# Layer 1 of a hybrid decoder step: transposed queries and keys leave PSUM in one copy

## The chip, the cores and the metric

The kernel runs on one core of a Trainium2 chip. The metric is the device time of one execution in microseconds. Four engines do the work here: TensorE (PE, with its weight loads shown as PEld), VectorE (DVE), ScalarE (ACT) and GpSimd (POOL); the queue of SyncE (SP) issues the DMAs. Matmul results land in PSUM, which ACT and DVE read; everything else lives in SBUF.

## The reference, cut to what matters

Layer 1 is stick-breaking attention with 16 heads of width 64 over 1024 prompt tokens (and 8 samples of 8 tokens, which go another way and matter little here).

```
u = h @ w_in
q = rms_norm(u[..., :SB_W].reshape(bsz, length, SB_HEADS, SB_DH), qn)
k = rms_norm(u[..., SB_W:2 * SB_W].reshape(bsz, length, SB_HEADS, SB_DH), kn)
...
z = jnp.einsum('bqhd,bkhd->bhqk', qi, k).astype(jnp.float32) * (dh ** -0.5) + bias_f
valid = k_pos[None, :] < pi[:, None]
log_1mb = jnp.where(valid, jax.nn.log_sigmoid(-z), 0.0)
rest = lax.cumsum(log_1mb, axis=3, reverse=True)
a = jnp.exp(jnp.where(valid, z + rest, -jnp.inf))
return jnp.einsum('bhqk,bkhd->bqhd', a.astype(v.dtype), v)
...
return (o * jax.nn.silu(g)) @ w_out, k, v
```

Every matmul operand is split into a high part in fp32r and a low part, the rest of it, so that products come out near full fp32 accuracy. Making such parts is what the code of this change does.

## The kernel before

Layer 0 takes the first 535 us, layer 1 the rest. Layer 1 goes over 8 pairs of heads (p = 0 to 7), and in each pair over four blocks of 256 tokens (m = 0 to 3). For each pair and block it does, on different engines at once:

- The projection of two row tiles of 128 tokens to this pair's q, k and v columns (`dense`, line 293, into PSUM tile `acc`), and of the gate columns (`dense_t`, line 315). ACT squares q and k (`sq`, L799) and copies v (L801), DVE sums (`ms`, L802), POOL takes the power -1/2 (`rs`, L804), and DVE scales q and k out of `acc` into SBUF (`qk`, L810), which frees `acc` for the next tile.
- `qk_p`, once per block: PE transposes q and k of both row tiles into a PSUM tile `tr` of 128x512 (L829). Then ten operations read `tr`: ACT makes four pieces of the queries' high part `qh` (L853, four operations on 64 partitions) and two pieces of the keys' high part into `kc` (L854, L855); DVE makes the two pieces of the queries' low part `ql` (L856, L857) and the two low pieces of the keys in `kc` (L858, L859). The function runs 32 times.
- The attention units, two heads by m + 1 key blocks: logits `z` on PE (L881), two sigmoids on ACT (`om` L884, `A` L885), on diagonal units a masking on POOL (L890), the running products by a scan on DVE (`run`, L908) and a product (L913 or L916). Then `A` is transposed by PE into another `tr` tile (L932), copied out as high part by ACT (`aT`, L934) and low part by DVE (L935), and multiplied with v on PE (`o`, L944).
- `gate_b`, once per block: it adds the two halves of `o` (ACT copies one half to `sh`, L954; DVE adds, L955, into `og`) and POOL multiplies with the gate (L956).
- The weights of the next pair: DMA into a ring of three raw tiles `wr`, high part on ACT or DVE (L219, L221), low part on POOL (L222). This falls into block 3 of a pair.

Each of the PSUM tiles `acc`, `tr`, `z` and `o` has two buffers. The order of the matmuls on PE is written by hand, by the times given to a timeline; the order on ACT, DVE, POOL and SP is made by a scheduler from the dependencies. Each engine runs its own queue strictly in order, so an instruction that waits holds all behind it.

Of the kernel before, what the change touches and what calls it, by code (L numbers as in the profile page):

```python
# [9 lines left out]
F32 = mybir.dt.float32  # L10
# [3 lines left out]
AF = mybir.ActivationFunctionType  # L14
# [62 lines left out]
def tile_hybrid_decoder(ctx, tc, x_prompt, x_sample, state_gla, cache_k, cache_v, page_table,  # L77
# [3 lines left out]
    nc = tc.nc  # L81
# [46 lines left out]
    def sb(pool, name, shape, dtype=F32, bufs=2, tag=None):  # L128
        return pools[pool].tile(shape, dtype, name=name, tag=tag or name, bufs=bufs)
# [532 lines left out]
    for h in range(GH):  # L662
# [3 lines left out]
        for c, (c_0, n) in enumerate(CH):  # L666
            st = {}
            G.append(st)
            if h == 0:
                a, b = QK0[c]  # L670
                la = LA0[c]
            else:
                a, b = i, i + 1
# [5 lines left out]
            for j, (key, out) in enumerate((("q", q_out), ("k", k_out))):  # L679
                lo, hi = a + (b - a) * 0.5 * j, a + (b - a) * 0.5 * (j + 1)  # L680
                dense_t(lo, hi, c_0, n, wqk,
                        lambda w, k, j=j: (w[k // 2], slice((k % 2) * 256 + j * 128, (k % 2) * 256 + j * 128 + 128)),
# [84 lines left out]
    K1 = {}  # L767
# [59 lines left out]
    def turn_qk(st, n, tr, slots):  # L827
        for j, x in enumerate(slots):
            nc.tensor.transpose(tr[:, x, :n], st["qk"][:n, 2 * j:2 * j + 2].rearrange("p a d -> p (a d)"), ident[:n, :n])  # L829
# [7 lines left out]
    def qk_p(sts, pair):  # L837

        tr = psum.tile([128, 4, 128], F32, name="tr")
        for x, st in enumerate(sts):
            turn_qk(st, 128, tr, (x, 2 + x))
        tr = tr.rearrange("p a s -> p (a s)")
        qp, kp, g = tr[:, :256], tr[:, 256:], K1["gains"]
        qh, kc = sb("at2", "qh", [128, 2, 256], F32R, NQ), sb("at2", "kc", [128, 2, 256], F32R, NKV)
        ql = K1["ql"][K1["turn"] % NQ]
        K1["turn"] += 1
        pair["q"].append((qh, ql))
        pair["k"].append(kc)  # L850
        up, dn = slice(0, 64), slice(64, 128)
        for dst, j, src in ((up, 0, up), (dn, 1, dn), (dn, 0, up), (up, 1, dn)):
            nc.scalar.activation(qh[dst, j], qp[src], AF.Copy, scale=g[src])  # L853
        nc.scalar.activation(kc[up, 0], kp[up], AF.Copy)  # L854
        nc.scalar.activation(kc[dn, 1], kp[dn], AF.Copy)  # L855
        nc.vector.scalar_tensor_tensor(ql[up, 0], qp[up], g[up], qh[up, 0], op0=OP.mult, op1=OP.subtract)  # L856
        nc.vector.scalar_tensor_tensor(ql[dn, 1], qp[dn], g[dn], qh[dn, 1], op0=OP.mult, op1=OP.subtract)  # L857
        nc.vector.tensor_sub(kc[dn, 0], kp[up], kc[up, 0])  # L858
        nc.vector.tensor_sub(kc[up, 1], kp[dn], kc[dn, 1])  # L859
# [87 lines left out]

    def gate_b(q, pair, p, m):
        po = q["po"]
        sh, og = sb("at2", "sh", [128, 256], F32, 1), sb("at2", "og", [128, 256], F32, 2)  # L950
        q["og"] = og
        for j in range(2):
            main, other = slice(64 * j, 64 * j + 64), slice(64 - 64 * j, 128 - 64 * j)
            nc.scalar.activation(sh[main], po[other, j], AF.Copy)  # L954
            nc.vector.tensor_add(og[main], po[main, j], sh[main])  # L955
        nc.gpsimd.tensor_mul(og, og, pair["g"][m])  # L956

    def tps(m):
# [30 lines left out]
    for p in range(PAIRS):  # L989
# [4 lines left out]
        def columns(t, i, span):  # L994
            st = {}
            dense(i, t, w, st, span, 384)
            e = i + span
            at(e + 0.02, qk_sums, st, p, t)
            at(e + C_SC, qk_scale, st, p, t)
            sts.append(st)  # L1000
            if t < NP:
                at(max(e + C_SC, open2), v_parts, st, t, pair)
            if t == NP:
                at(e + C_TS, qk_s, st, p)
            elif t % 2 == 1:
                at(max(e + C_T, open2 + 0.01 * t), qk_p, sts[t - 1:], pair)
            at(max(e + C_T, open2) + 0.2, kv_store, st, p, t)
            return e
# [8 lines left out]
        for m in range(NP // 2):  # L1017
            i = columns(2 * m, i, 0.75)
            i = columns(2 * m + 1, i, 0.75)
            ready = max(i + UNIT0, open2 + 0.5)  # L1020
            if m < NP // 2 - 1:
                i = gates(m, i, 0.5)
            else:
                i = gates(m, i, 0.625)
                i = columns(NP, i, 0.5)
            q = {}
            units = [(j, c) for j in range(2) for c in range(m, -1, -1)]
            for x, (j, c) in enumerate(units):
                u = {}
                z0 = max(free, ready)  # L1030
                free = z0 + PACE
                at(z0, logits, u, pair, p, m, c, j)
                at(z0 + L_STICK, stick, u, pair, m, c, j)
                at(z0 + L_TURN, turn, u, m, c)
                at(z0 + L_AV, weigh, u, q, pair, c, j, x == 0, x == len(units) - 1)
            at(z0 + L_AV + 0.05, gate_b, q, pair, p, m)
            at(z0 + L_AV + 0.35, store_b, q, p, m)
            if p == PAIRS - 1:
                st = {}
                for g in range(4):  # L1040
                    n = 2 if g < 3 else 1
                    at(i + 0.1 + 0.05 * g, load_h, st, m, g, n)
                    at(i + 0.6 + 0.05 * g, take_h, st, m, g, n)
# [203 lines left out]
```

## Time and profile before

| what | value |
|---|---|
| runs before, median (range), n = 3 | 1372.65 us (1367.76 to 1372.9) |
| the profiled execution, its own time | 1375.27 us |
| its span in the profile | 1373.6 us |
| busy, PE / PEld | 1282.8 us (93%) / 1140.3 us (83%) |
| busy, DVE / ACT / POOL | 1012.5 us (74%) / 709.7 us (52%) / 587.0 us (43%) |
| DMA | 115.82 MB, mean 84 GB/s |

The busy shares are means over the whole run. PE is the busiest engine in every stage; what a change in layer 1 is worth is read from what PE waits for there, and from what the other engines wait for just before.

### The profile page before, as it was taken

The numbers are of one execution on the slowest core, as the hardware profiler recorded it, in microseconds if no ns is written. First come the engines' busy times: TensorE is split into PE (matmuls) and PEld (weight loads), VectorE is DVE, ScalarE is ACT, GpSimd is POOL, SyncE is SP. The second block draws the span as 40 slices with busy tenths as digits, with TensorE's granted clock in tenths as the row PEclk, the third lists the DMA queues.
The fourth block names the chain that finished last, engine by engine and source line by source line (L and its number), as shares of the span: only waits on it lengthen the run. The fifth ranks groups of instructions, "written<-read, shape, count | busy, mean of one in ns | idle before, by whom it ended". The sixth has DMA issues, their size and how long they took to land.

```text
span 1373.6 us, 23656 instructions
## 1 busy us (share of the span) xinstructions
PE 1282.8 (93%) x8025; PEld 1140.3 (83%) x8025; DVE 1012.5 (74%) x2047; ACT 709.7 (52%) x1640; POOL 587.0 (43%) x1101
## 2 busy tenths in 40 slices
PE   6999999999999998989989899898998989989998
PEld 5788888888878788989889898898998988877666
DVE  7858759668564457788888988789788898986443
ACT  6446245352441134566756667566666667763221
POOL 6223223223231216465655846557466574543000
PEclk9999999999999999999999999999999999999999
DMA  6311402304246423020110201102012022134762
GB/s 195 92 32 43 137 20 68 108 32 133 91 129 213 145 101 104 18 81 18 58 42 22 79 17 55 47 24 80 16 41 63 23 89 68 32 121 155 249 245 88
DMA packets 118459, 115.82 MB, mean 84 GB/s; under 512 B 11003, under 2 KB 97923, under 8 KB 118339
## 3 DMA queue, kind: packets, MB, share of 16 engines
q1 hardware_dynamic: 118338, 114.31, 27.2%
q8 instruction: 64, 1.05, 0.3%
q14 instruction: 57, 0.46, 0.1%
HBM read 83.61 MB, written 30.67 MB: 83 GB/s over the span
## 4 chain that ended last, share of the span: by engine, by line
PE 55%; DVE 18%; POOL 9%; ACT 7%; issue 7%; DMA 3%; SPq 1%; POOLq 0%; ACTq 0%; DVEq 0%
PE acc L293 31%; PE acc L315 7%; DVE run L908 4%; PE z L881 3%; PE tr L932 3%; PE o L944 2%; POOL wlo L222 2%; POOL rs L804 2%; ACT qh L853 2%; DVE whi L221 2%; PE o L544 1%; DVE aT L935 1%; DVE wr L217 1%; POOL v L819 1%; PE o L1154 1%
## 5 line engine op out<-in xcount | busy, mean ns | idle before, releaser
L293 PE MATMUL acc<-whi,h 128*128 128x512 f32 (+1 forms) x1728 | 538.7, 374 | 10.1 <-DVE qk L810 7.9
L293 PEld LDWEIGHTS acc<-whi,h 128*128 128x128 f32 x1728 | 313.5, 189 | 41.1 <-ACT sh L954 4.2
L293 PE MATMUL acc<-wlo,h 128*128 128x512 f32 (+1 forms) x864 | 322.5, 373 | 3.9 <-DVE wlo L222 2.5
L315 PE MATMUL acc<-h,whi 128*128 128x256 f32 (+5 forms) x832 | 193.5, 318 | 10.3 <-DVE g L512 5.1
L222 POOL TENSOR_TENSOR wlo<-wr,whi 128x512 fp32r<-128x512 f32 x98 | 139.1, 1422 | 123.5 <-DVE whi L221 93.2
L293 PEld LDWEIGHTS acc<-wlo,h 128*128 128x128 f32 x864 | 162.8, 188 | 22.7 <-DVE wlo L222 3.2
L908 DVE TENSOR_TENSOR_SCAN run<-om,run 128x256 f32<-128x256 f32 x192 | 146.7, 802 | 11.0 <-ACT om L884 10.5
L315 PEld LDWEIGHTS acc<-h,whi 128*128 128x128 f32 (+2 forms) x832 | 141.3, 189 | 15.1 <-DVE g L512 6.0
L934 ACT ACTIVATE aT<-tr 128x512 fp32r<-128x512 f32 (+1 forms) x160 | 88.9, 556 | 103.9 <-PE tr L932 90.2
L884 ACT ACTIVATE om<-z,bias 128x512 f32<-128x512 f32 (+1 forms) x160 | 103.3, 646 | 52.6 <-PE z L881 43.1
L932 PE MATMUL tr<-ident,A 128*128 128x128 f32 x576 | 91.5, 277 | 39.3 <-POOL v L819 18.3
L315 PE MATMUL acc<-h,wlo 128*128 128x256 f32 (+2 forms) x392 | 123.8, 316 | 0.5 <-POOL wlo L222 0.5
L293 PE MATMUL acc<-w,h 128*128 128x384 f32 (+1 forms) x480 | 122.6, 365 | 0.7 <-DVE qk L810 0.7
L932 PEld LDWEIGHTS tr<-ident,A 128*128 128x128 f32 x576 | 69.5, 142 | 55.1 <-POOL run L903 19.4
L935 DVE TENSOR_TENSOR aT<-tr,aT 128x512 fp32r<-128x512 f32 (+1 forms) x160 | 100.8, 630 | 9.1 <-ACT aT L934 6.8
L944 PE MATMUL o<-aT,v 128*128 128x256 f32 x640 | 105.0, 286 | 0.0
L885 ACT ACTIVATE A<-z,bias 128x512 f32<-128x512 f32 (+1 forms) x160 | 102.4, 640 | 0.0
L944 PEld LDWEIGHTS o<-aT,v 128*128 128x128 f32 x640 | 97.2, 194 | 1.8 <-DVE aT L935 1.1
L908 DVE TENSOR_TENSOR_SCAN run<-om 128x128 f32<-128x128 f32 (+1 forms) x128 | 85.0, 695 | 13.6 <-POOL om L890 13.6
L881 PE MATMUL z<-kc,qh 128*128 128x256 f32 x320 | 86.1, 290 | 7.3 <-DVE kc L858 7.3
L804 POOL TENSOR_TENSOR rs<-ms,half_exp 128x4 f32<-128x4 f32 (+1 forms) x72 | 83.9, 1166 | 20.3 <-DVE ms L802 18.8
L293 PEld LDWEIGHTS acc<-w,h 128*128 128x128 f32 x480 | 82.2, 189 | 7.2 <-issue 2.5
(274 smaller groups left out, 2531.7 us busy)
## 6 DMA issues: line engine op xcount, KB each, us to landing
wr<-in_w_in_b_dram SPq DMA_DIRECT2D x64, 256.0 KB, 3.0
wr<-in_w_in_a_dram SPq DMA_DIRECT2D x32, 256.0 KB, 3.2
kp<-in_cache_k_dram SPq DMA_DIRECT2D x16, 512.0 KB, 5.0
vp<-in_cache_v_dram SPq DMA_DIRECT2D x16, 512.0 KB, 4.5
o_d<-og SPq DMA_DIRECT2D x60, 128.0 KB, 1.8
x<-in_x_prompt_dram SPq DMA_DIRECT2D x8, 512.0 KB, 4.8
wr<-in_w_in_a_dram SPq DMA_DIRECT2D x32, 128.0 KB, 3.7
n<-in_state_gla_dram SPq DMA_DIRECT2D x8, 512.0 KB, 3.9
```

Source lines behind the costliest of these rows:

```text
L222: engine.tensor_sub(e.lo[:, :m], raw[:, :m], e.hi[:, :m])
L293: nc.tensor.matmul(st["ps"][:x.shape[1], :n], x, (w[k].hi if part == 0 else w[k].lo)[:, :n], start=first, stop=last)
L315: nc.tensor.matmul(st[key][:x.shape[1], :n], x, y, start=first, stop=last)
L804: nc.gpsimd.tensor_tensor(st["rs"][:n], ms[:n], half_exp[:n], op=OP.pow)
L881: nc.tensor.matmul(out, lhs, rhs, start=x == 0, stop=x == len(mm) - 1)
L884: nc.scalar.activation(u["om"][:, v0:], z[:, v0:], AF.Sigmoid, scale=-1.0, bias=K1["bias"][:, 1, hd:hd + 1])
L885: nc.scalar.activation(u["A"][:, v0:], z[:, v0:], AF.Sigmoid, bias=K1["bias"][:, 0, hd:hd + 1])
L908: nc.vector.tensor_tensor_scan(run[:, a, n - 1::-1], rev, rev, init, op0=OP.mult, op1=OP.bypass)
L932: nc.tensor.transpose(tr[:, x], u["A"][:, col:col + 128], ident)
L934: nc.scalar.activation(hi[:, v0:], tr[:, v0:], AF.Copy)
L935: nc.vector.tensor_sub(lo[:, v0:], tr[:, v0:], hi[:, v0:])
L944: nc.tensor.matmul(q["po"][:, j], vs, part[:, x * 256:(x + 1) * 256], start=first and n == 0, stop=last and n == 3)
```

## The change

`qk_p` copies the whole `tr` tile once to an SBUF tile `both` on ACT, and the ten operations read `both`. To make room in SBUF, `gate_b` loses its tile `sh`: ACT copies the half of `o` straight into `og`, and DVE adds in place.

```diff
@@ qk_p
         for x, st in enumerate(sts):
             turn_qk(st, 128, tr, (x, 2 + x))
-        tr = tr.rearrange("p a s -> p (a s)")
-        qp, kp, g = tr[:, :256], tr[:, 256:], K1["gains"]
+        both = sb("at2", "both", [128, 512], F32, 1)
+        nc.scalar.activation(both, tr.rearrange("p a s -> p (a s)"), AF.Copy)
+        qp, kp, g = both[:, :256], both[:, 256:], K1["gains"]
@@ gate_b
-        sh, og = sb("at2", "sh", [128, 256], F32, 1), sb("at2", "og", [128, 256], F32, 2)
+        og = sb("at2", "og", [128, 256], F32, 2)
         q["og"] = og
         for j in range(2):
             main, other = slice(64 * j, 64 * j + 64), slice(64 - 64 * j, 128 - 64 * j)
-            nc.scalar.activation(sh[main], po[other, j], AF.Copy)
-            nc.vector.tensor_add(og[main], po[main, j], sh[main])
+            nc.scalar.activation(og[main], po[other, j], AF.Copy)
+            nc.vector.tensor_add(og[main], po[main, j], og[main])
```

Lines behind the diff's first place are one higher in the changed kernel (L856 becomes L857, L932 becomes L933, and so on). The order of PE's 6801 instructions does not change.

On ACT, in the third block of a pair, the queue reads as follows before the change; what stands in brackets are the engines whose semaphores an instruction waits for.

```order
L885 ACTIVATE A<-z,bias 128x512
L853 ACTIVATE qh<-tr,gains 64x256 [waits PE_49]
L853 ACTIVATE qh<-tr,gains 64x256 x3
L854 ACTIVATE kc<-tr 64x256
L855 ACTIVATE kc<-tr 64x256
L934 ACTIVATE aT_7570<-tr 128x384 [waits PE_49,Activation_49,Pool_49]
```

And with the change:

```order
L886 ACTIVATE A<-z,bias 128x512
L845 ACTIVATE both<-tr 128x512 [waits PE_49]
L854 ACTIVATE qh<-both,gains 64x256 [waits Activation_49]
L854 ACTIVATE qh<-both,gains 64x256 x3
L855 ACTIVATE kc<-both 64x256
L856 ACTIVATE kc<-both 64x256
L935 ACTIVATE aT_7579<-tr 128x384 [waits PE_49,Pool_49]
```

One instruction is added ahead of the six, and the first of the six waits for it.

On DVE, at the same place, the first `ql` waits for ACT and the other three behind it for nothing further before the change:

```order
L916 TENSOR_TENSOR A<-A,run 128x512 [waits DVE_49,Activation_49,Pool_49]
L856 SCALAR_TENSOR_TENSOR ql_5786<-tr,gains,qh 64x256 [waits PE_49,Activation_49]
L857 SCALAR_TENSOR_TENSOR ql_5786<-tr,gains,qh 64x256
L858 TENSOR_TENSOR kc<-tr,kc 64x256
L859 TENSOR_TENSOR kc<-tr,kc 64x256
L935 TENSOR_TENSOR aT_7571<-tr,aT_7570 128x384 [waits Activation_49]
```

With the change each of the four has a wait of its own:

```order
L917 TENSOR_TENSOR A<-A,run 128x512 [waits DVE_49,Activation_49,Pool_49]
L857 SCALAR_TENSOR_TENSOR ql_5786<-both,gains,qh 64x256 [waits Activation_49]
L858 SCALAR_TENSOR_TENSOR ql_5786<-both,gains,qh 64x256 [waits Activation_49]
L859 TENSOR_TENSOR kc<-both,kc 64x256 [waits Activation_49]
L860 TENSOR_TENSOR kc<-both,kc 64x256 [waits Activation_49]
L936 TENSOR_TENSOR aT_7580<-tr,aT_7579 128x384 [waits Activation_49]
```

On PE, in the last block of a pair, the second transpose of an `A` behind a `qk_p` (the one that gets its buffer of `tr` back) reads so before:

```order
L932 MATMUL tr<-ident,A 128x128 [waits DVE_49,PE_49,Pool_49]
L932 MATMUL tr<-ident,A 128x128 x2
```

And with the change:

```order
L933 MATMUL tr<-ident,A 128x128 [waits DVE_49,Activation_49,Pool_49]
L933 MATMUL tr<-ident,A 128x128 x2
```

It now waits for ACT as well; DVE and POOL stay, since `A` comes from there.

## Rows read from the trace of the kernel before

**Rows 1.** Who waited for whom, PE, 535 to 1260 us: total, times, longest.

```profile
PE tr L932 <- POOL v L819: 18.3, 6, 3.1
PE tr L932 <- DVE kc L859: 11.9, 8, 1.8
PE acc L293 <- DVE qk L810: 8.6, 10, 1.7
PE z L881 <- DVE kc L858: 7.3, 10, 1.4
PE tr L932 <- ACT sq L799: 4.5, 7, 0.9
```

**Rows 2.** Who waited for whom, DVE, the same stretch.

```profile
DVE ql L856 <- ACT kc L855: 45.8, 24, 4.7
```

**Rows 3.** Timeline, block 0 of pair 3: start, us, instruction, [idle before it].

```profile
793.29 1.92 ACT L853 ACTIVATE qh<-tr,gains 64x256 fp32r<-64x256 f32 x4 [1.32 <-PE tr L829]
...
795.61 0.38 ACT L855 ACTIVATE kc<-tr 64x256 fp32r<-64x256 f32 x1
...
796.01 0.60 ACT L934 ACTIVATE aT<-tr 128x512 fp32r<-128x512 f32 x1
796.02 0.48 DVE L856 SCALAR_TENSOR_TENSOR ql<-tr,gains,qh 64x256 fp32r<-64x256 f32 x1 [2.38 <-ACT kc L855]
...
797.45 0.43 DVE L859 TENSOR_TENSOR kc<-tr,kc 64x256 fp32r<-64x256 f32 x1
...
797.90 0.69 DVE L935 TENSOR_TENSOR aT<-tr,aT 128x512 fp32r<-128x512 f32 x1
798.02 0.63 PE L932 MATMUL tr<-ident,A 128*128 128x128 f32 x4 [0.58 <-ACT sq L799]
```

**Rows 4.** Timeline, block 2 of the same pair.

```profile
833.89 0.38 ACT L854 ACTIVATE kc<-tr 64x256 fp32r<-64x256 f32 x1
...
835.71 0.42 DVE L858 TENSOR_TENSOR kc<-tr,kc 64x256 fp32r<-64x256 f32 x1
...
836.27 0.36 PE L881 MATMUL z<-kc,qh 128*128 128x256 f32 x1 [0.56 <-DVE kc L858]
```

**Rows 5.** Timeline, block 3 of the same pair.

```profile
854.13 1.32 POOL L222 TENSOR_TENSOR wlo<-wr,whi 128x512 fp32r<-128x512 f32 x1
854.24 0.47 DVE L856 SCALAR_TENSOR_TENSOR ql<-tr,gains,qh 64x256 fp32r<-64x256 f32 x1
...
855.66 0.42 DVE L859 TENSOR_TENSOR kc<-tr,kc 64x256 fp32r<-64x256 f32 x1
...
856.23 0.52 PE L932 MATMUL tr<-ident,A 128*128 128x128 f32 x3 [1.46 <-DVE kc L859]
...
856.77 1.30 POOL L222 TENSOR_TENSOR wlo<-wr,whi 128x512 fp32r<-128x512 f32 x1 [1.17 <-ACT whi L219]
...
857.18 2.07 DVE L908 TENSOR_TENSOR_SCAN run<-om,run 128x256 f32<-128x256 f32 x2
```

**Rows 6.** Timeline at the end of the same block 3.

```profile
871.02 0.87 PE L932 MATMUL tr<-ident,A 128*128 128x128 f32 x3 [3.06 <-POOL v L819]
```

**Rows 7.** Instructions of ACT by shape: busy us, mean ns, idle before.

```profile
L1110 ACT ACTIVATE KT<-tr 128x512 f32<-128x512 f32 x16 | 9.6, 598 | 31.3 <-PE tr L1107 31.2
...
L965 ACT ACTIVATE h<-og 128x256 fp32r<-128x256 f32 x4 | 1.7, 418 | 1.5 <-POOL og L956 1.5
```

**Rows 8.** Busy us from 815.30 to 825.50, by engine: PE, PEld, DVE, ACT, POOL.

```profile
815.30:825.50 10.20, 10.11 (x74) 9.79 (x74) 9.96 (x23) 6.70 (x16) 6.99 (x18) 1.00 0.10 31
```

**Rows 9.** Line 810, all: ns min/median/max, first and last start.

```profile
L810 DVE TENSOR_TENSOR qk<-acc,rs x64: 393/425/426, 527.6 to 1195.9; 128x256 f32<-128x256 f32 x64
...
L810 DVE TENSOR_TENSOR qk<-xr,rs x8: 406/1172/1178, 600.8 to 1215.2; 64x256 f32<-64x256 f32 x8
```

**Rows 10.** The page's group of full scans on DVE (busy us, mean ns).

```profile
L908 DVE TENSOR_TENSOR_SCAN run<-om,run 128x256 f32<-128x256 f32 x192 | 146.7, 802 | 11.0 <-ACT om L884 10.5
```

**Rows 11.** Who waited for whom, PE, 1255 us to the end.

```profile
PE tr L1107 <- DMA kp<-in_cache_k_dram: 3.8, 4, 1.8
```

## The prediction

> **What bounds the kernel now.** I read the busy shares first. PE is the busiest engine over the run (93%), so the matmuls alone would take most of the time, and the change leaves their number and order as they are. What it can move is the time in which PE waits, in layer 1 alone. So the second view is who waited for whom, on PE, over layer 1 [rows 1]. Its five largest lines add up to 50.6 us in some 725, and two of them name the low key pieces of `qk_p` outright: 11.9 us in which a transpose waits for L859, and 7.3 us in which logits wait for L858. A third, 4.5 us in seven waits, names ACT's `sq`, and here the reader should look closer. In the timeline of that place [rows 3] PE starts the transposes at 798.02. They need a free `tr`, and the last reader of the buffer that comes round is L859, which ends at 797.88, 0.14 us before. In blocks 2 and 3, where the view names L858 and L859, PE starts 0.14 and 0.15 us behind them [rows 4, 5]. `sq` has nothing to do with `tr`; it only ended a moment later. So all three lines, 23.7 us, hang on `qk_p`.
>
> The third view is DVE's own waits. Its largest by far is the first `ql`, 45.8 us in 24 waits, for ACT's last key piece [rows 2]. That is odd, since `ql` needs only the first piece of `qh`. In block 0 the six ACT pieces run from 793.29 to 795.99, and `ql` starts 0.03 us behind the last of them, after 2.38 us of idling [rows 3]. DVE does not read `tr` while ACT does. [...] So the ten readers of `tr` are one chain of some 4.6 us (793.29 to 797.88), and the buffer is taken throughout.
>
> **The change, part by part.**
>
> The copy. It has the shape of L1110, a 128x512 fp32 copy out of PSUM: 0.60 us [rows 7]. The six pieces behind it then read SBUF. The nearest row is L965, 128x256 from SBUF, 0.418 us [rows 7], against 0.38 for a key piece [rows 3]. That is up to 0.04 us more for each, 0 to 0.24 us for six; I take 0.15, and 0.03 for the first one's wait for the copy, as `ql` shows it for another engine. ACT's key pieces, and everything behind them on ACT, come 0.8 us later (bounds 0.6 and 0.9). For ACT that is 32 x 0.8 = 26 us more work at a busy share of 52%.
>
> `tr` is free 0.60 us after the transposes instead of 4.6. The seven waits of block 0 go: PE comes to them at 798.02 - 0.58 = 797.44, and the buffer is free at 793.9. Gain 4.5 us.
>
> The logits of block 2. Each DVE piece now waits for its own ACT piece alone, as the order shows. The first ACT key piece ends at 834.27 [rows 4]; 0.8 later is 835.07, the DVE piece starts 0.03 behind it and ends at 835.52, against 836.13 now: 0.61 us earlier, enough for the wait of 0.56. Of the ten waits I take seven as of this size, 3.9 us, and let the three that share the other 3.4 us gain no more than 0.61 each. Gain 5.7 us.
>
> DVE behind the pieces, in blocks 0 and 1. Its next instruction (L935) needs ACT's `aT`, which ends 0.8 us later, at 797.41, and the last DVE piece, which ends at 795.99 + 0.8 + 0.03 + 0.43 = 797.25. So it starts at 797.44 and not at 797.90, 0.46 us earlier. In block 1 DVE then has no rest for ten microseconds (9.96 of 10.20 us busy [rows 8]), up to the sums that lead to `qk`, for which PE waits 8.6 us in ten waits [rows 1]. I take 0.4 us for eight of them, 3.2 us; bounds 0 and 4.6.
>
> The last block is different. There DVE does not wait for ACT: it comes to `ql` late, at 854.24, without idling, while POOL works on weights [rows 5]. The wait of 1.46 us goes from the transposes, but DVE is what is late, and PE then waits for its next products, and again 3.06 us at the block's end [rows 6]. I count none of the 11.9 us; the upper bound is half of it, 6 us.
>
> And there is a cost. The four DVE pieces so far have one input in PSUM, and ran at 0.42 to 0.49 us beside POOL's L222 (854.13 to 855.45) [rows 5]. Now both inputs lie in SBUF. What that means is seen at line 810 [rows 9]: `qk` out of PSUM never took more than 0.426 us in 64 times, while the same operation with both inputs in SBUF, which stands in this same block, took 1.172 in the median. So `ql` would start at 855.45, the four would end 1.84 us later at 857.29, and the scans, which follow 1.10 us behind (856.08 to 857.18), would start at 858.39. Two scans without disturbance take 2 x 0.80 [rows 10], so they end at 859.99 and not at 859.25. That is 0.74 us; I take 0.8. It is nothing if the four come before L222 and POOL bears the wait, and 0.74 + 1.30 = 2.0 us if the second L222, which asks at 856.77, gets in between the four. With 0.8 us in seven pairs (pair 7 has no further pair to prepare) the loss is 5.6 us. It lies on the path: it ends in the wait at 871.02 [rows 6], on a POOL that is behind the scans.
>
> [...]
>
> `gate_b` only writes to another tile. ACT's second half there still waits for DVE's first, and `og` has two buffers, a block apart: nothing. On SP's queue some loads of cached keys at the end of the run come earlier; the waits for them are 3.8 us [rows 11]. I take 0.
>
> Sum: 4.5 + 5.7 + 3.2 - 5.6 = 7.8 us off the profiled execution's own 1375.27, or 0.57%. That execution is 0.2% above the median of the runs, 1372.65; 0.57% off the median is 1364.9, and I say 1365.
>
> **The rivals.**
>
> [...]
>
> [...]
>
> The gains are hidden: the end of a pair is set by POOL's chain of weights, and the 3.06 us [rows 6] grow by what was saved. 1372. Against: POOL starts on the weights behind scans that follow PE's logits, so an earlier PE brings it forward too.
>
> Slower: ACT becomes the bound. Its 26 us come on the path, with 10.2 us gained on PE: 1388. For it: ACT is in order, and `aT`, the sigmoids and `sq` stand behind the pieces. Against: `aT` has 797.90 - 796.61 = 1.29 us until DVE takes it [rows 3], more than 0.8. It decides where that slack is missing in more than 10.2 / 0.8 = 13 of the 32 blocks.
>
> **How the numbers follow.** 0.45 for the forecast (its own range 1360 to 1371), 0.17 for the cheap port, 0.18 for the dear one, 0.10 for hidden gains, 0.10 for ACT. 0.5% is 6.9 us, about what a measurement here can tell from no change. Faster by more: all of the cheap port and two thirds of the forecast, 0.47. Slower by more: ACT, and a fourth of the dear port, 0.15. The rest, 0.38, is no change. The range leaves out the ACT case and the far half of the cheap port: 1354 to 1377.
>
> **What would show it.** Right: DVE's wait at `ql` falls from 45.8 us to well under half, split over four smaller ones; PE's lines for L858 and for `sq` nearly vanish; the DVE pieces stay near 0.45 us in blocks 0 to 2 and grow past 1 us in block 3; the wait at a pair's end [rows 6] stays or grows. Wrong, and faster: pieces as short in block 3 as elsewhere. Wrong, and slower: PE waiting for `aT` or `sq`, or DVE waiting for `aT` longer than the 0.03 us of a handover.

## The result, and the profile after

The changed kernel takes 1386.84 us (median of 5 runs, 1382.09 to 1390.0), against 1372.05 for the kernel before, measured beside it: ratio 1.0112, 95% interval 1.0085 to 1.0139. It is slower by 1.1%, where a gain of 0.57% was forecast, and lies outside the range. The profiled execution has a span of 1388.3 us, against 1373.6.

What the change was to do to the waits, it did. First PE, from 535 to 1275 us, who waited for whom (total, times, longest):

```profile
PE tr L933 <- DVE A L914: 24.0, 9, 3.4
PE acc L293 <- DVE qk L810: 17.5, 11, 2.6
PE o L945 <- DVE aT L936: 13.4, 8, 1.7
PE acc L293 <- DVE xr L725: 2.9, 1, 2.9
...
PE z L882 <- DVE kc L859: 1.0, 2, 0.7
```

The three lines that hung on `qk_p` [rows 1] have become one of 1.0 us. But the wait for `qk` went from 8.6 us to 17.5, and a new line of 13.4 us has come, in eight waits: the products `o` of block 3 for the low part of `aT`. Most of the 24.0 us, seven of the nine waits, are the wait at a pair's end [rows 6], now called by another name and a little longer (3.39 us in pair 3, the last row of the timeline after, below). The same view for DVE:

```profile
DVE kc L859 <- ACT kc L855: 21.1, 24, 1.0
...
DVE aT L936 <- ACT aT L935: 17.1, 38, 2.5
DVE run L909 <- POOL om L891: 12.6, 33, 0.6
...
DVE ql L857 <- ACT qh L854: 9.1, 13, 2.4
```

The wait of 45.8 us at `ql` [rows 2] is split as foreseen. But DVE's wait for ACT's `aT`, which the prediction named as a sign of a loss, has grown from 6.8 us in 8 waits to 17.1 in 38. And ACT, by shape (busy us, mean ns, idle before):

```profile
L854 ACT ACTIVATE qh<-both,gains 64x256 fp32r<-64x256 f32 x128 | 64.9, 507 | 3.1
...
L845 ACT ACTIVATE both<-tr 128x512 f32<-128x512 f32 x32 | 19.2, 599 | 23.1 <-PE tr L829 22.6
...
L855 ACT ACTIVATE kc<-both 64x256 fp32r<-64x256 f32 x32 | 13.4, 418 | 0.4
...
L856 ACT ACTIVATE kc<-both 64x256 fp32r<-64x256 f32 x32 | 13.3, 415 | 0.8
```

The copy takes 0.60 us, a query piece 0.507, a key piece 0.42. Before, out of PSUM, the same view has:

```profile
L853 ACT ACTIVATE qh<-tr,gains 64x256 fp32r<-64x256 f32 x128 | 60.2, 470 | 23.5 <-PE tr L829 21.8
...
L855 ACT ACTIVATE kc<-tr 64x256 fp32r<-64x256 f32 x32 | 12.2, 380 | 0.6
L854 ACT ACTIVATE kc<-tr 64x256 fp32r<-64x256 f32 x32 | 12.1, 378 | 0.4
```

So six pieces cost 0.22 us more. With the copy's 0.60 and a handover of 0.03 (in block 0 of pair 3 the copy ends at 797.56 and the first piece starts at 797.59) ACT is 0.9 us late where I said 0.8: its last key piece there ends 4.23 us behind the start of the transposes, 3.34 before.

To see where the time went I counted from the first transpose of one `qk_p` (L829) to that of the next, by the start times in the trace. The table holds the sums over the pairs, in us (eight intervals in the first three columns, seven in the last; the tail behind the last call is left out). All kernels of the experiments are in it; the numbers in brackets are theirs. The last column moves by 3 to 5 us between kernels that hardly differ there (216.9 before and 213.7 in (3), 216.2 in (4) and 211.3 in (11)). In the kernel before this interval took 32.1 us in pair 3, where the granted clock stood at 0.50 for 6.8 us (870.2 to 877.0), and 30.8 in pair 4, where it did so for 3.4 (959.0 to 962.4). So the column is read with care.

| kernel | block 0 to 1 | 1 to 2 | 2 to 3 | 3 to next | median, us |
|---|---|---|---|---|---|
| before | 151.3 | 154.2 | 142.8 | 216.9 | 1372.05 |
| changed | 148.4 | 167.8 | 137.4 | 220.6 | 1386.84 |
| (1) changed, order of before | 147.9 | 156.3 | 137.8 | 217.4 | 1370.22 |
| (2) no copy, order of changed | 152.3 | 162.4 | 142.2 | 218.4 | 1383.03 |
| (3) no copy, `gate_b` in place | 151.4 | 154.2 | 142.8 | 213.7 | 1371.35 |
| (4) copy in blocks 0, 2 | 148.1 | 154.2 | 137.7 | 216.2 | 1362.36 |
| (5) changed, `og` in its old place | 148.3 | 158.7 | 137.4 | 218.2 | 1378.08 |
| (6) copy twice, order of before | 153.0 | 161.2 | 142.8 | 221.2 | 1386.41 |
| (7) copy in 0, 2, 3, order of before | 147.8 | 154.2 | 137.8 | 220.1 | 1369.34 |
| (8) as (7), DVE reads PSUM in block 3 | 146.8 | 154.2 | 137.8 | 215.2 | 1363.41 |
| (9) changed, DVE's order of before | 147.8 | 158.7 | 137.3 | 221.3 | 1375.57 |
| (10) no copy, `og` in its new place | 151.7 | 159.2 | 142.7 | 214.2 | 1376.75 |
| (11) as (4), order of before | 147.9 | 154.2 | 137.8 | 211.3 | 1362.97 |
| (12) kc's high pieces on DVE | 145.0 | 149.1 | 139.3 | 215.7 | 1354.92 |

The gains in blocks 0 and 2 are there (2.9 and 5.4 us). Block 1 has lost 13.6 us, by far the largest loss. The tail is not even either: it took 173.6 us before and 179.1 after, but 170.0 in (1) and 171.4 in (2). Of all the profiled kernels only (5), at 180.2, is like the changed one; the others lie between 168.5 and 173.6. So the tail is long where the copy meets DVE's new queue, in one execution of each. Part of the 5.5 us is PE's wait for cached keys, 6.9 us instead of the 3.8 of [rows 11]; the rest was not followed up.

In pair 3 block 1 reads as follows before the change, first DVE, then POOL, then PE (start, us, instruction, [idle before it]):

```profile
820.45 0.42 DVE L810 TENSOR_TENSOR qk<-acc,rs 128x256 f32<-128x256 f32 x1
820.82 0.43 DVE L908 TENSOR_TENSOR_SCAN run<-om 128x128 f32<-128x128 f32 x1
821.16 0.39 DVE L955 TENSOR_TENSOR og<-o,sh 64x256 f32<-64x256 f32 x1
821.47 0.67 DVE L908 TENSOR_TENSOR_SCAN run<-om 128x256 f32<-128x256 f32 x1
822.07 0.59 DVE L913 TENSOR_TENSOR A<-A,run 128x128 f32<-128x128 f32 x2
822.69 0.43 DVE L955 TENSOR_TENSOR og<-o,sh 64x256 f32<-64x256 f32 x1
823.15 0.56 DVE L935 TENSOR_TENSOR aT<-tr,aT 128x384 fp32r<-128x384 f32 x1
...
821.41 1.57 POOL L812 TENSOR_TENSOR kout<-qk,kn 128x128 f32<-128x128 f32 x1
...
823.20 0.74 POOL L956 TENSOR_TENSOR og<-og,gt 128x256 f32<-128x256 f32 x1
...
827.60 1.29 PE L293 MATMUL acc<-w,h 128*128 128x384 f32 x6 [0.65 <-DVE qk L810]
```

The same place after:

```profile
823.57 0.42 DVE L810 TENSOR_TENSOR qk<-acc,rs 128x256 f32<-128x256 f32 x1
823.91 0.41 DVE L956 TENSOR_TENSOR og<-o,og 64x256 f32<-64x256 f32 x1
824.36 1.17 DVE L909 TENSOR_TENSOR_SCAN run<-om 128x128 f32<-128x128 f32 x2
825.55 0.43 DVE L956 TENSOR_TENSOR og<-o,og 64x256 f32<-64x256 f32 x1
826.01 1.17 DVE L914 TENSOR_TENSOR A<-A,run 128x128 f32<-128x128 f32 x2
827.22 0.56 DVE L936 TENSOR_TENSOR aT<-tr,aT 128x384 fp32r<-128x384 f32 x1
...
824.95 0.83 POOL L812 TENSOR_TENSOR kout<-qk,kn 128x128 f32<-128x128 f32 x1
...
826.06 0.84 POOL L957 TENSOR_TENSOR og<-og,gt 128x256 f32<-128x256 f32 x1
...
831.54 1.93 PE L293 MATMUL acc<-w,h 128*128 128x384 f32 x6 [1.79 <-DVE qk L810]
...
876.73 0.87 PE L933 MATMUL tr<-ident,A 128*128 128x128 f32 x3 [3.39 <-DVE A L914]
```

The reader is to see two things. `gate_b`'s two additions (`og`) have moved forward: the first stood between the scans and now stands ahead of both, the second stood behind the two products `A` and now stands ahead of them. So POOL's product of `og`, which waits for the second addition, now starts at 826.06, beside the products `A`, and these take 1.17 us instead of 0.59. (Before, the products ran beside POOL's `kout`, and it was `kout` that was drawn out, to 1.57 us where it takes 0.83 after.) From the start of this `qk` to that of the low part of `aT` it takes 3.65 us instead of 2.70, and PE's wait for the `qk` behind it is 1.79 us instead of 0.65. Of these 0.95 us some 0.6 are the products' own. In the experiments below it is the place that decides: with the additions in the new place (the changed kernel, (2) and (10)) the second product takes 0.96 us in each of pairs 1 to 5, with the old one (before, (1), (5) and (9)) 0.41.

Right behind that wait PE's granted clock falls, to 0.50 for 3.4 us, in five of the eight pairs. Busy us of PE, PEld, DVE, ACT and POOL, then the granted clock, in pair 3 of the changed kernel; the row behind the "..." is the same stretch of pair 4, where it doesn't fall:

```profile
831.90:835.30 3.40, 3.40 (x14) 3.30 (x13) 2.88 (x7) 0.61 (x2) 1.33 (x4) 0.50 0.10 24
835.40:845.00 9.60, 9.60 (x66) 9.26 (x66) 6.74 (x14) 7.57 (x16) 3.41 (x11) 1.00 0.06 20
...
921.00:924.40 3.40, 3.40 (x24) 3.37 (x25) 3.17 (x8) 1.41 (x3) 1.33 (x5) 1.00 0.08 22
```

In 3.4 us at a granted clock of 0.50 PE gets 14 matmuls done where it does 24 in 3.4 us at 1.00. Block 1 takes 21.87 us in pair 3 and 20.31 in pair 4, 19.41 and 19.44 before; so a fall costs some 1.55 us here, and without it 0.9 us are lost.

### The profile page after: what moved, and what is told of

Read it like the earlier page. It is cut to its first block, busy times and chain, and to the rows that moved or that the text cites. A ratio compares the mean times of both kernels' runs of the same rounds, so it can differ in the third digit from the quotient of the medians.

```text
span 1388.3 us, 23638 instructions
## 1 busy us (share of the span) xinstructions
PE 1290.7 (93%) x8025; PEld 1149.1 (83%) x8025; DVE 1035.1 (75%) x2047; ACT 732.2 (53%) x1672; POOL 583.2 (42%) x1101
## 4 chain that ended last, share of the span: by engine, by line
PE 57%; DVE 24%; issue 6%; ACT 4%; POOL 4%; DMA 4%; SPq 1%; DVEq 0%; POOLq 0%; ACTq 0%
PE acc L293 34%; PE acc L315 7%; DVE run L909 6%; PE z L882 3%; PE o L945 3%; PE tr L933 3%; DMA kp<-in_cache_k_dram 2%; DVE whi L221 2%; DVE aT L936 2%; DVE A L914 2%; DVE A L917 1%; PE o L544 1%; DVE wr L217 1%; POOL rs L804 1%; ACT qh L854 1%
## 5 line engine op out<-in xcount | busy, mean ns | idle before, releaser
L293 PE MATMUL acc<-whi,h 128*128 128x512 f32 (+1 forms) x1728 | 543.3, 377 | 19.2 <-DVE qk L810 15.7
L222 POOL TENSOR_TENSOR wlo<-wr,whi 128x512 fp32r<-128x512 f32 x98 | 139.2, 1423 | 126.5 <-DVE whi L221 93.3
L909 DVE TENSOR_TENSOR_SCAN run<-om,run 128x256 f32<-128x256 f32 x192 | 142.7, 780 | 9.2 <-ACT om L885 7.8
L945 PE MATMUL o<-aT,v 128*128 128x256 f32 x640 | 107.8, 289 | 13.4 <-DVE aT L936 13.4
L933 PE MATMUL tr<-ident,A 128*128 128x128 f32 x576 | 93.4, 282 | 26.6 <-DVE A L914 24.0
L936 DVE TENSOR_TENSOR aT<-tr,aT 128x512 fp32r<-128x512 f32 (+1 forms) x160 | 100.3, 630 | 18.4 <-ACT aT L935 17.1
L945 PEld LDWEIGHTS o<-aT,v 128*128 128x128 f32 x640 | 97.8, 195 | 17.5 <-DVE aT L936 16.8
L933 PEld LDWEIGHTS tr<-ident,A 128*128 128x128 f32 x576 | 72.3, 144 | 39.4 <-POOL v L819 23.5
L909 DVE TENSOR_TENSOR_SCAN run<-om 128x128 f32<-128x128 f32 (+1 forms) x128 | 94.9, 781 | 12.9 <-POOL om L891 12.6
L804 POOL TENSOR_TENSOR rs<-ms,half_exp 128x4 f32<-128x4 f32 (+1 forms) x72 | 83.3, 1157 | 18.4 <-DVE ms L802 16.6
```

Of the source, the lines that this page charges most:

```text
L222: engine.tensor_sub(e.lo[:, :m], raw[:, :m], e.hi[:, :m])
L293: nc.tensor.matmul(st["ps"][:x.shape[1], :n], x, (w[k].hi if part == 0 else w[k].lo)[:, :n], start=first, stop=last)
L804: nc.gpsimd.tensor_tensor(st["rs"][:n], ms[:n], half_exp[:n], op=OP.pow)
L909: nc.vector.tensor_tensor_scan(run[:, a, n - 1::-1], rev, rev, init, op0=OP.mult, op1=OP.bypass)
L933: nc.tensor.transpose(tr[:, x], u["A"][:, col:col + 128], ident)
L936: nc.vector.tensor_sub(lo[:, v0:], tr[:, v0:], hi[:, v0:])
```

## The experiments

Every kernel was timed beside the kernel before on the same chip; the ratios are to that. The kernel before took 1370.9 to 1372.05 us in the median of each group, so the times can be compared with each other to about 1 us.

**Is it the copy, or the order that the scheduler made?** The diff adds nothing to `gate_b` that would move `og`. But the scheduler lays out DVE, ACT, POOL and SP anew, and with ACT later it chose another order on all four. Two kernels cross the one with the other. The order is pinned by edges that hold the issue order and wait for nothing:

```diff
+    for e, order in orders.items():
+        for a, b in zip(order, order[1:]):
+            tc.add_manual_dep(made[e][b], made[e][a].name, mybir.DependencyInfo(
+                mybir.DependencyClass.NoSync, mybir.DependencyReason.DATA), reason="order")
```

Here `orders` is the other kernel's order, engine by engine, and `made` the instructions as the program issues them.

(1) Copy, order of before:

> The changed kernel, copy and all, but the scheduler's order of the kernel before is pinned on DVE, ACT, POOL and SP (edges of issue order alone, each instruction behind the one that stood ahead of it; the copy goes straight ahead of its pieces on ACT). Theory ORDER (the loss comes from the order that the scheduler chose anew: og's additions ahead of the products A in block 1, weight work ahead of the last key piece on ACT): the predicted gains come through and the loss goes, 1360 to 1368 us, block 1 to 2 at 19.4 us or less. Theory LATE (ACT is 0.9 us later in each block, so the masks and scans of block 1 are late whatever the order): 1383 to 1390, block 1 to 2 near 21.8 us as in the changed kernel.

Measured: 1370.22 us, ratio 0.9986 (0.9972 to 1.0). (2) No copy, order of the changed kernel:

> The kernel before, without the copy, but with the order of the changed kernel pinned on DVE, ACT, POOL and SP. ORDER: slower than before, 1380 to 1395 us, block 1 to 2 well above 19.4 us. LATE: no loss, 1369 to 1375 us, block 1 to 2 at 19.4 us.

Measured: 1383.03 us, ratio 1.0079 (1.006 to 1.0097). ORDER holds in both: the order alone makes the kernel before slower by 0.8%, and without it the copy doesn't lose. LATE as the main cause falls. ORDER missed in one point: the predicted gains did not come through with the old order, 1370 instead of 1360 to 1368, and block 1 took 19.7 us instead of 19.4.

The two causes do not simply add. With the old order the copy gives 0.1%; with the new one it costs another 0.3% (from ratio 1.0079 to 1.0112). In (2) block 1 takes 20.3 us in pairs 1 to 6, and the granted clock falls there in pair 7 alone; with the copy it falls in five pairs (its mean over the profiled execution is 0.986 in (2) and 0.983 in the changed kernel). So the 17 us between (1) and the changed kernel are what the order costs where the copy is there too.

(3) The other half of the diff:

```diff
-            nc.scalar.activation(sh[main], po[other, j], AF.Copy)
-            nc.vector.tensor_add(og[main], po[main, j], sh[main])
+            nc.scalar.activation(og[main], po[other, j], AF.Copy)
+            nc.vector.tensor_add(og[main], po[main, j], og[main])
```

> The kernel before with the edit in gate_b alone (ACT's half goes to og, no tile sh). Its order on all engines is that of before. Both ORDER and LATE: no change, 1370 to 1375 us. Theory GATE (that og is read and written in place costs something): slower, up to the 1387 us of the changed kernel.

Measured: 1371.35 us, ratio 0.9992 (0.9978 to 1.0005). No change; GATE falls.

**Which place of the order?** (5) The changed kernel in its own order, but for `gate_b`'s two additions on DVE in block 1 of pairs 1 to 7 (shown here by tile; the run pins the whole queue by number):

```diff
-og, run, run, og, A, A, aT
+run, og, run, A, A, og, aT
```

> The changed kernel with its own order on all engines, but for one place: in block 1 of pairs 1 to 7 gate_b's two additions on DVE stand where they stood before (the first between the two scans, the second behind the two products A). [...] Rival ELSEWHERE (the other new places, such as the diagonal A behind the low part of aT, or ACT's weight work ahead of the last key piece): 1383 to 1389 us.

Measured: 1378.08 us, ratio 1.0046 (1.003 to 1.0062). In pairs 1 to 5 block 1 takes 19.9 to 20.2 us, and the clock falls there no more (one fall stays, in pair 7; the mean is 0.989). ELSEWHERE falls. So this one place is worth 0.66%, some 9 us of the 17 between the changed kernel and (1). (10) The converse, the same two additions moved forward in the kernel before:

> The kernel before, without the copy and in its own order, but for gate_b's two additions in block 1 of pairs 1 to 7, which stand where the changed kernel has them: one ahead of both scans, one ahead of both products A. Theory OG (their place costs by itself, since POOL's product og then runs beside the second A): block 1 to 2 near 20.3 us as with the whole new order, 1375 to 1380 us. Rival BOTH (it costs only where ACT is late too, as in the changed kernel): block 1 to 2 stays at 19.4 us and the time at 1369 to 1373 us.

Measured: 1376.75 us, ratio 1.0039 (1.0025 to 1.0053). OG holds, BOTH falls; the size is smaller than said, block 1 takes 20.1 us and not 20.3. The wait for `qk` in block 1 of pair 3 is 1.37 us (before: 0.65):

```profile
828.98 1.28 PE L293 MATMUL acc<-w,h 128*128 128x384 f32 x6 [1.37 <-DVE qk L810]
```

(9) The rest of the order, by engine:

> The changed kernel with the order of before on DVE alone; ACT, POOL and SP keep the order that the scheduler chose anew. With the two additions of gate_b alone put back the run was at 1378 us, with all four engines put back at 1370. Theory DVE (what is left of the loss also sits in DVE's queue: the diagonal A, the last qk and the scans of other blocks): 1368 to 1373 us. Rival OTHERS (it sits in ACT's weight work ahead of the last key piece in block 3, in POOL's queue, or in the order of loads on SP at the run's end): 1375 to 1380 us.

Measured: 1375.57 us, ratio 1.0027 (1.0013 to 1.0041). It is OTHERS more than DVE: from (5) to (9) DVE's other places give 0.19%, which the intervals hardly part from nothing, and from (9) to (1) the order on ACT, POOL and SP gives 0.41%. (In the trace of (9) these three queues are not quite those of the changed kernel: eight places on POOL, two on SP and one on ACT differ, all of them in block 3 or behind it.) Which of the three it is was not tried apart. The table and the traces narrow it down: block 1 is the same in (5) and (9), 158.7 us, and 2.4 us longer than in (1): mostly 0.2 us a pair, and 1.7 in pair 7, where the clock falls. In pairs 1 to 7 the only difference between the queues there is that POOL's `rs` stands ahead of the second `v` instead of behind it. So 2.4 of the 5 to 6 us point to POOL's queue, by elimination and not by a run of its own.

**What is the copy itself worth, block by block?** (4) The copy in blocks 0 and 2 alone:

```diff
-        both = sb("at2", "both", [128, 512], F32, 1)
-        nc.scalar.activation(both, tr.rearrange("p a s -> p (a s)"), AF.Copy)
+        both = tr.rearrange("p a s -> p (a s)")
+        if len(pair["k"]) in (0, 2):
+            src, both = both, sb("at2", "both", [128, 512], F32, 1)
+            nc.scalar.activation(both, src, AF.Copy)
```

> The change with the copy in blocks 0 and 2 of each pair alone; blocks 1 and 3 read PSUM as before. The scheduler's order is that of before in blocks 0, 1 and 3, but for one swap on DVE in block 2 (low part of aT ahead of a scan). ORDER and LATE both: the gains of block 0 (3.0 us over the run) and block 2 (5.4 us) stay, the losses of block 1 and 3 go: 1372 less 8.4, 1362 to 1366 us. Theory SPILL (a copy in block 0 makes ACT late for block 1 too, since PE comes earlier to it than ACT and DVE do): the wait for qk in block 1 grows by what block 0 gained, and the time is 1366 to 1372 us.

Measured: 1362.36 us, ratio 0.9935 (0.9914 to 0.9957). Blocks 0 and 2 give what they were said to give, block 1 is as before, SPILL falls. (11) The same with the order of before pinned:

> The copy in blocks 0 and 2 alone, with the order of before pinned on DVE, ACT, POOL and SP. The run with the scheduler's own order had one swap on DVE in block 2 and took 1362 us. If that swap (low part of aT ahead of a scan) matters: 2 us or more away from 1362; if not, 1360 to 1364 us.

Measured: 1362.97 us, ratio 0.9934 (0.9918 to 0.995). The swap doesn't matter, nor do some other places that the traces show to be new in (4), nine on POOL and one each on DVE and SP. The pins cost nothing by themselves either: block 1 takes 19.4 us in (11) as it does before. With block 3 added, (7), and with DVE's four pieces there out of PSUM, (8):

```diff
+        if len(pair["k"]) == 4:
+            qp, kp = whole[:, :256], whole[:, 256:]
         nc.vector.scalar_tensor_tensor(ql[up, 0], qp[up], g[up], qh[up, 0], op0=OP.mult, op1=OP.subtract)
```

> The copy in blocks 0, 2 and 3, block 1 as before, in the order of before. Beside the run with the copy in blocks 0 and 2 (1362 us) it prices block 3. Theory PORT (the prediction: ql of two SBUF inputs starts behind POOL's weight product and takes 1.5 us instead of 0.47, the scans behind it are late, 0.8 us in each of seven pairs): 1366 to 1370 us. Rival EVEN (the transposes' wait of 1.46 us goes and the late scans give it back elsewhere, about nothing in sum): 1360 to 1364 us.

> As the run with the copy in blocks 0, 2 and 3, but in block 3 DVE's four pieces take their source from PSUM (tr) and ACT's six from the copy. PORT: the first ql in block 3 takes 0.47 us instead of 1.5, DVE's four pieces end about 1 us earlier, and the time is 1359 to 1364 us, 3 us or more under the run with all ten pieces from the copy. EVEN: no difference to it beyond 2 us. Theory LATEDVE (block 3 hangs on when DVE comes to the pieces, not on how long they take): the pieces are short and the transposes behind wait 1.5 us for tr again, 1362 to 1366 us.

Measured: (7) 1369.34 us, ratio 0.9985 (0.9972 to 0.9999); (8) 1363.41 us, ratio 0.9944 (0.9924 to 0.9964). The copy in block 3 costs 6.4 us beside (11), and 5.9 of them go when DVE reads PSUM. PORT holds, EVEN falls. Block 3 of pair 3 in (7), DVE and POOL:

```profile
855.06 1.50 DVE L859 SCALAR_TENSOR_TENSOR ql<-both,gains,qh 64x256 fp32r<-64x256 f32 x1
856.59 0.48 DVE L860 SCALAR_TENSOR_TENSOR ql<-both,gains,qh 64x256 fp32r<-64x256 f32 x1
...
854.95 1.33 POOL L222 TENSOR_TENSOR wlo<-wr,whi 128x512 fp32r<-128x512 f32 x1
```

And in (8):

```profile
853.42 0.47 DVE L861 SCALAR_TENSOR_TENSOR ql<-tr,gains,qh 64x256 fp32r<-64x256 f32 x1
853.92 0.49 DVE L862 SCALAR_TENSOR_TENSOR ql<-tr,gains,qh 64x256 fp32r<-64x256 f32 x1
```

In (7) `ql` starts at 855.06 and is done at 856.56, 0.28 us behind POOL's L222 (856.28): it took 1.03 us longer than in (8). LATEDVE is half right too: the transposes of (8) do wait for `kc` again, 12.3 us in eight waits, as before [rows 1], and still it is the faster one.

**And block 1, in the order of before?** There the copy loses 0.3 us in each of pairs 1 to 6 (19.71 against 19.42). In (1), block 1 of pair 3, whose transposes start at 809.10, POOL's mask and then DVE:

```profile
814.63 0.41 POOL L891 TENSOR_SCALAR_AFFINE_SELECT om<-om 128x256 f32<-128x256 f32 x1 [1.87 <-ACT om L885]
...
813.99 0.69 DVE L936 TENSOR_TENSOR aT<-tr,aT 128x512 fp32r<-128x512 f32 x1 [0.19 <-ACT aT L935]
815.07 1.17 DVE L909 TENSOR_TENSOR_SCAN run<-om 128x128 f32<-128x128 f32 x2 [0.39 <-POOL om L891]
```

Before, with the transposes at 811.92:

```profile
816.56 0.41 POOL L890 TENSOR_SCALAR_AFFINE_SELECT om<-om 128x256 f32<-128x256 f32 x1 [0.98 <-ACT om L884]
...
817.18 0.69 DVE L935 TENSOR_TENSOR aT<-tr,aT 128x512 fp32r<-128x512 f32 x1
817.79 0.41 DVE L908 TENSOR_TENSOR_SCAN run<-om 128x128 f32<-128x128 f32 x1
```

Counted from the transposes, DVE takes the low part of `aT` 0.37 us earlier with the copy (4.89 against 5.26), as the prediction had it. But POOL's mask comes 0.89 us later (5.53 against 4.64), since `om` on ACT does, and the scan behind it starts at 5.97 instead of 5.87: the lead is lost in a wait of 0.39 us that was not there. That is 0.10 of the 0.30 us. The rest comes a little later, at the first two products `A`. In (1), DVE and POOL:

```profile
816.48 0.88 DVE L914 TENSOR_TENSOR A<-A,run 128x128 f32<-128x128 f32 x2
...
816.41 0.47 POOL L820 TENSOR_TENSOR v<-v,v 128x128 fp32r<-128x128 f32 x1
```

And before:

```profile
819.25 0.63 DVE L913 TENSOR_TENSOR A<-A,run 128x128 f32<-128x128 f32 x2
...
819.40 1.01 POOL L804 TENSOR_TENSOR rs<-ms,half_exp 128x4 f32<-128x4 f32 x1 [0.94 <-DVE ms L802]
```

The products start only 0.05 us later (7.38 against 7.33) but take 0.88 us instead of 0.63: POOL's `v`, late behind its mask, now runs beside the first of them, where POOL had idled until 0.15 us behind their start. (6) doubles what is late:

```diff
         nc.scalar.activation(both, tr.rearrange("p a s -> p (a s)"), AF.Copy)
+        nc.scalar.activation(both, tr.rearrange("p a s -> p (a s)"), AF.Copy)
```

> The changed kernel in the order of before (as in the first run), with ACT's copy of tr made twice, so that all behind it on ACT is 0.6 us later once more. Theory LATE (what is left of the loss in block 1 with the old order, 0.30 us a pair, is ACT's lateness, which reaches the scans through om and POOL's mask with no slack left): the scan behind the mask starts 0.6 us later, block 1 to 2 is 20.3 us (19.7 + 0.6), and the run is 5 to 12 us longer than with one copy, 1375 to 1382 us. [...]

Measured: 1386.41 us, ratio 1.0117 (1.0097 to 1.0137). In pair 3 block 1 takes 20.34 us, as LATE said: what ACT is late passes on in full (0.63 us over the 19.71 of (1), for a copy of 0.60). That the scans have slack, which would have left block 1 near 19.7 us, falls. The products `A` held up beside POOL's `v` are what the rows above show for 0.25 of the 0.30 us, and they take 0.88 us in (12) too. So lateness sets the pace in block 1; what the meeting with POOL costs by itself no run separates. But the run lost more than said: blocks 0 and 2 lose 0.6 us each as well. Of 32 x 0.60 = 19.2 us of copies, some 16 us came on the path. (12) goes the other way and takes 0.84 us off ACT in blocks 0 to 2, to a place where DVE idles (in the changed kernel 9.1 us ahead of `ql`, 21.1 ahead of `kc`):

```diff
-        nc.scalar.activation(kc[up, 0], kp[up], AF.Copy)
-        nc.scalar.activation(kc[dn, 1], kp[dn], AF.Copy)
+            high = [nc.vector.tensor_copy(kc[up, 0], kp[up]), nc.vector.tensor_copy(kc[dn, 1], kp[dn])]
```

> The copy in blocks 0, 1 and 2, and in these blocks the two high key pieces are made by DVE out of the copy, in the time in which it idles ahead of ql, instead of by ACT; block 3 as before; else the order of before on DVE, ACT, POOL and SP. ACT's chain is 0.84 us shorter than in the changed kernel, so aT and om come about as early as without the copy. Theory LATE, from its other side (0.6 us more on ACT cost 0.62 us in each of blocks 0 to 2, so 0.84 us less give something back in each): block 0 under 18.4, block 1 under 19.3, block 2 under 17.0 us, and 1350 to 1358 us. Rival FLOOR (below the pace of the copy in blocks 0 and 2 another chain binds, PE's own work or DVE's): block 0 at 18.65, block 1 at 19.4, block 2 at 17.15 us, and 1360 to 1364 us as with the copy in blocks 0 and 2.

Measured: 1354.92 us, ratio 0.9874 (0.9852 to 0.9896), the fastest of all. Its block 1 of pair 3, POOL and DVE, with the transposes at 803.65:

```profile
808.18 0.41 POOL L901 TENSOR_SCALAR_AFFINE_SELECT om<-om 128x256 f32<-128x256 f32 x1 [0.87 <-ACT om L895]
...
805.09 0.60 DVE L858 CAST kc<-both 64x256 fp32r<-64x256 f32 x2
805.72 0.48 DVE L863 SCALAR_TENSOR_TENSOR ql<-both,gains,qh 64x256 fp32r<-64x256 f32 x1
...
808.62 1.17 DVE L919 TENSOR_TENSOR_SCAN run<-om 128x128 f32<-128x128 f32 x2 [0.27 <-POOL om L901]
```

The mask is at 4.53 and the scan at 4.97 from the transposes, earlier than in either kernel, and block 1 takes 18.7 us. LATE holds there, and for the time of the run. Block 0, at 18.47 us, lies between the two (under 18.4 by LATE, 18.65 by FLOOR), and block 2 is longer than either said: 17.39 us, 0.25 more than with the copy and ACT's key pieces. Why was not looked into.

## Why the prediction was wrong

**The step that failed** is one that the part on the change does not have. It costs what the diff edits, takes `gate_b` at "nothing", and the only moves that it names are some loads on SP's queue, at 0. It had seen that PE's order stays, and the traces show PE's matmuls in one and the same order throughout. That the order on the other engines is laid out anew, and so changes in places that the diff does not touch, got no term and no rival. By (1), (2), (5) and (10) it is the cause of the loss: from ratio 0.9986 to 1.0112, some 17 us with the copy in place, and 0.8% without it. About 9 of the 17 are `gate_b`'s additions in block 1, which its edit alone, (3), does not move; some 5 to 6 are the order on ACT, POOL and SP.

**The terms**, against the runs with the order of before:

- Block 0, the seven waits of the transposes: 4.5 us said; the sums give 151.3 less 147.9, 3.4 us.
- Block 2, the logits: 5.7 us said, 5.0 measured (142.8 less 137.8).
- "DVE behind the pieces, in blocks 0 and 1": 3.2 us said. Here the sign was wrong. DVE does come earlier to the low part of `aT`, by 0.37 us, but what it does next waits for `om`, over ACT and POOL's mask, and ACT is later by 0.9: the lead turns into 0.10 us of delay, and POOL's `v`, late with the mask, then holds up a product for 0.25. Block 1 loses 2.1 us (156.3 less 154.2). The trap was to follow one engine's queue forward without its other inputs.
- Block 3, DVE's pieces beside POOL's L222: a loss of 5.6 us said, 5.9 measured between (7) and (8), 6.4 for the block. The price was nearly right, but no run shows its term, a `ql` that starts only when L222 has ended: in (7) `ql` starts at 855.06, 0.11 us behind the start of L222 and 1.22 ahead of its end, and takes 1.50 us. As foretold, the transposes' wait went over to PE's next products: the line of 13.4 us above, 16.0 in (1).
- ACT's lateness: 0.8 us said, 0.9 measured. In the traces a query piece took 37 ns more out of SBUF than out of PSUM (507 against 470), a key piece 35 to 40 (418 and 415 against 378 and 380). I had taken 25 ns a piece.

In sum these terms give 3.4 + 5.0 - 2.1 - 6.4, about nothing, and (1) measures 1.1 us under the kernel before. So even with the old order the forecast of 7.8 us would have failed, by the third term above all.

**The rivals.** "ACT becomes the bound", 1388 us, came nearest in number and was not what happened: by (1) the copy with the order held costs nothing in sum. By (6) and (12), though, it named what lies next to the path. Its condition, the slack of `aT`, was the wrong one to watch; it is the slack of `om`, ahead of POOL's mask, that is missing. The cheap and the dear case of block 3 in the chances, 0 and 14 us in seven pairs, lie on both sides of the 5.9 us that (7) and (8) show.

**Open** is why the granted clock falls behind the wait of 1.79 us in pair 3 and not behind that of 1.81 in pair 4, where the rest of the tail's 5.5 us comes from, and which of ACT's, POOL's and SP's new places costs what is left of the 5 to 6 us beyond POOL's 2.4 in block 1.

## What to carry to other kernels

Where a scheduler orders the engines, a change in one place is two changes. Compare the orders of the whole program, not of the edited function alone, and pin the old order once to learn what the edit is worth by itself; here the edit was worth -0.1% and the new order +1.3% on top of it, 0.8% without it. The early release of the buffer was paid for on the engine that made it early: the same copy gained 0.66% in blocks 0 and 2, gave most of it back in block 3, and stood at 1.3% (without block 3) once two of the pieces had moved from the late engine to the one that idled.

## What the runs showed of the hardware

Which engine takes longer where DVE and POOL work side by side changes in these runs from case to case. Beside POOL's product of `og` DVE's two products `A` took 1.17 us instead of 0.59; beside `kout` they kept their 0.59 and `kout` took 1.57 us instead of 0.83; the first two products `A` of a block 1 took 0.88 us beside POOL's `v` in (1) and (12), and 0.63 before; a `ql` with both inputs in SBUF took 1.50 us beside POOL's L222 in (7), and 0.47 with one input in PSUM before [rows 5]. The order of their starts did not tell which: L222 started 0.11 us ahead of `ql` and took 1.33 us, as it did before [rows 5] (1.32), and `ql` was drawn out; `kout` started 0.66 us ahead of the products (821.41 against 822.07) and was drawn out itself, as far as starts on POOL can be read from a trace. Not expected was how far a loss of 0.95 us on DVE goes: with the wait behind it (1.79 us instead of 0.65) and a fall of the granted clock to 0.50 for 3.4 us, block 1 lost 2.5 us in four pairs (21.87 against 19.41 in pair 3).
